# Strassen's scheme for the merge gates of a decoder layer, with the gates kept in DRAM and the up projections turned round

## The chip, the core and the metric

The kernel runs on one core of a Trainium2 chip. The core has a matrix engine (TensorE; PE in the profile, PEld its weight loads), a vector engine (VectorE, DVE), a scalar engine (ScalarE, ACT), a general one (GpSimd, POOL) and a queue engine (SyncE, SP) that here only starts transfers; POOL starts some as well. Each runs its own instructions in the order in which the program issues them; they meet at semaphores. On-chip memory has 128 partitions. Matmul results arrive in eight banks of 128 x 512 float32 values, which the kernel names in four kinds of two: g, s, t, o. The metric is the device time of one execution, in microseconds (us).

## The reference

512 tokens, 2048 channels, one layer. What matters here:

```python
h = rms_norm(x, norm_g[l])
proj = h @ w_in[l]
q, kv, g_logits, z_a, uv, z_b, merge_logits = jnp.split(proj, SPLIT_IDX, axis=-1)
...
o_a = nsa_attention(q, ...) * jax.nn.silu(z_a)                       # 1024 wide
o_b = spatial_gating(uv, ...) * jax.nn.silu(z_b)                     # 1024 wide
g_a, g_b = jnp.split(jax.nn.sigmoid(merge_logits), 2, axis=-1)       # 2048 wide each
merged = g_a * (o_a @ w_up_a[l]) + g_b * (o_b @ w_up_b[l])
x = x + merged @ w_out[l]
x = x + jax.nn.sigmoid(x @ w_ple_gate[l]) * (p[l] @ w_ple[l])
return rms_norm(x, final_g)
```

`merge_logits` is the product of h (512 x 2048) with the last 4096 columns of `w_in`: the largest product of the layer.

## The kernel before

Every projection is a `Job`, and one generator, `gemm` (L170), issues the matmuls of all jobs in the order in which `add_job` listed them. `fill(n)` lets it go n yields further, `finish(name)` until a job is done. Float32 is kept by a split: each operand is a high part (rounded to the matmul's type) and a low part (the rest), and each product is three matmuls: high x high, high x low, low x high. Weights come by SP's queue in 512 KB loads into a ring of three (`raw`, L137); ScalarE casts the high part (`high`, L98, from L150), VectorE subtracts for the low part (`low`, L104, from L162), in pieces ("subs") of 128 x 512. `split_to` does this two subs ahead of the matmuls (`state["ahead"]`), the cast one more. The buffers of high parts are four, of low parts three.

A job of kind "T" has 128 columns of weights as the stationary operand and all 512 tokens moving: its result has channels on partitions. A sub holds four blocks of 128 rows (`per_sub`), so 4 x 3 = 12 matmuls. A job of kind "N" has 128 tokens stationary and 512 columns of weights moving: tokens on partitions, a sub is one block of rows, four token tiles, again 12 matmuls.

Two lists carry other work. What stands in `deferred` is issued at the next `flush()`. What stands in `background` is taken off one or two entries (`state["pops"]`) at each sub, after the split of the sub two ahead and before the matmuls of the present one.

The stages in order: PLE products and norms; keys, values and compression; attention, with q and za jobs woven in; then vn (L410), u (L412) and zb (L414) for the gated MLP; then for each of 16 blocks of 128 channels the gates `ma`, `mb` (2048 deep) and the up projections `ua`, `ub` (1024 deep) (L457 to L461); `wo`; `pg`. o_a is split into `oa_h`, `oa_l` after the attention (background, L967), o_b into `ob_h`, `ob_l` by `evac_zb` (L399). The gate's sigmoid is taken as tanh, with the factor 0.5 applied later: `evac_gate` (L426) puts tanh into `sig` tiles, `evac_up` (L447) forms (tanh + 1) x product on VectorE and adds the two branches on POOL into `m32` (channels on partitions), and `merged_split` (L438) splits that into `act_h`, `act_l`, which until then held h. `x2` is the same memory as `m32`, reloaded from x.

In the u stage the work is ordered by hand: the layer norm's pieces (`aggregate` and eight `affine`, L1009) go through `background`, one per sub, until the list is empty (L1025); then after each u job the four spatial-gating matmuls (L1034), the add on VectorE (L1037) and the multiplication on POOL (L1039), with `fill(3)` in between.

Of the kernel before, what the change touches and what calls it, by code (L numbers as in the profile page):

```python
# [20 lines left out]
P = 128  # L21
# [15 lines left out]
class Job:  # L37
# [5 lines left out]

    def __init__(self, name, kind, w, c0, cols, kt, act, evac, banks=None, tail=0):
        self.name, self.kind, self.w, self.c0, self.cols, self.kt = name, kind, w, c0, cols, kt
        self.act, self.evac, self.banks, self.tail = act, evac, banks, tail
        self.per_sub = max(1, 512 // cols)
        self.per_load = 2 * self.per_sub


@with_exitstack
def kernel(ctx: ExitStack, tc: tile.TileContext, x, p, norm_g, w_in,
# [67 lines left out]

    def add_job(job):
        first = 0
        while first < job.kt:
            n = min(job.per_load, job.kt - first)
            loads.append((job, first, n))
            for k in range(first, first + n, job.per_sub):
                subs.append((job, k, min(job.per_sub, first + n - k), len(loads) - 1))
            first += n
        jobs.append(job)

    raw, parts = {}, {}
    state = {"loads": 0, "high": 0, "low": 0, "ahead": 0, "more": 1, "pops": 2}

    def load_to(i):
        while state["loads"] <= min(i, len(loads) - 1):
            job, k0, n = loads[state["loads"]]
            t = stream.tile([P, n, job.cols], F32, tag="raw", name="raw")  # L137
            nc.sync.dma_start(t, job.w[k0 * P:(k0 + n) * P, job.c0:job.c0 + job.cols]
                              .rearrange("(k p) c -> p k c", p=P))
            raw[state["loads"]] = (t, k0)  # L140
            state["loads"] += 1

    def split_to(i, more=1):
        while state["high"] <= min(i + more, len(subs) - 1):
            job, k, n, li = subs[state["high"]]
            t, k0 = raw[li]
            if k >= job.kt - job.tail:
# [3 lines left out]
            src = t[:, k - k0:k - k0 + n]  # L151
            high(hi, src)
            parts[state["high"]] = [hi, None, src]
            state["high"] += 1
        while state["low"] <= min(i, len(subs) - 1):
            job, k, n, li = subs[state["low"]]
            pt = parts[state["low"]]
            if k >= job.kt - job.tail:
# [5 lines left out]
            li = subs[state["low"] - 1][3]  # L164
            if state["low"] == len(subs) or subs[state["low"]][3] != li:
                load_to(li + 3)
# [3 lines left out]
    def gemm():  # L170
        si = 0
        for job in jobs:
            if job.kind == "T":
# [162 lines left out]
    spill = dram.tile([S, D], F32, name="spill")  # L336

# [61 lines left out]
    def evac_zb(ft):  # L399
        def f(ps):  # L400
# [5 lines left out]
            split(ob_h[:, ft], ob_l[:, ft], t, 0.5)  # L406
# [9 lines left out]
    oa = {}  # L416

    def oa_act(k):
        return oa["h"][:, k], oa["l"][:, k]

    def ob_act(k):
        return ob_h[:, k], ob_l[:, k]

    merge_tiles = {}

    def evac_gate(f, n):  # L426
# [9 lines left out]
    split_done = set()  # L436

    def merged_split(f):  # L438
        def e():
            split(act_h[:, f], act_l[:, f], merge_tiles["m"][:, f], 0.5)  # L440
            split_done.add(f)
            if len(split_done) == KT:
                for tt in range(TT):
                    nc.gpsimd.dma_start(x2[:, tt], x[tt * P:tt * P + P])
        return e

    def evac_up(f, n):  # L447
        def e(ps):
            t = merge_tiles[n]
            nc.vector.scalar_tensor_tensor(out=t, in0=t, scalar=1.0, in1=ps, op0=ALU.add, op1=ALU.mult)  # L450
            if n == 1:
# [656 lines left out]
```

## Time and profile before

| | |
|---|---|
| median of 3 runs | 1649.08 us (1649.03 to 1649.33) |
| the profiled execution, in all | 1649.7 us |
| its span, first to last instruction | 1648.0 us |
| granted TensorE clock, mean over the span | 0.998 |
| bytes moved | 168.02 MB, 102 GB/s on average |
| u jobs begin / zb jobs begin | 579.0 / 673.2 us |
| gates and up projections begin / wo begins | 760.4 / 1282.4 us |

The span is shorter than an execution by what lies around the first and the last instruction. A line of a group gives its source line, engine, operation, output and inputs, shapes and count, then busy time and the mean of one, then the engine's idle time ahead of it and what ended most of that. Matmuls overlap, so the duration of one is not its cost: cost is a stretch of the span divided by the matmuls in it.

### The profile page before, as it was taken

The numbers are of one execution on the slowest core, as the hardware profiler recorded it, in microseconds if no ns is written. First come the engines' busy times: TensorE is split into PE (matmuls) and PEld (weight loads), VectorE is DVE, ScalarE is ACT, GpSimd is POOL, SyncE is SP. The second block draws the span as 40 slices with busy tenths as digits, with TensorE's granted clock in tenths as the row PEclk, the third lists the DMA queues.
The fourth block names the chain that finished last, engine by engine and source line by source line (L and its number), as shares of the span: only waits on it lengthen the run. The fifth ranks groups of instructions, "written<-read, shape, count | busy, mean of one in ns | idle before, by whom it ended". The sixth has DMA issues, their size and how long they took to land.

```text
span 1648.0 us, 20570 instructions
## 1 busy us (share of the span) xinstructions
PE 1634.8 (99%) x7821; PEld 1368.2 (83%) x7821; DVE 748.7 (45%) x1500; ACT 616.5 (37%) x1241; POOL 114.6 (7%) x145
## 2 busy tenths in 40 slices
PE   9999999999999999999999999999999999999997
PEld 8889988888888888888888888888888888888886
DVE  6544378988873363343322222223223433333335
ACT  6433356666653232233222222222223322223335
POOL 1200000110120001000000000000000000000001
PEclk9999999999999999999999999999999999999999
DMA  8422421122124333343333333333333533363333
GB/s 318 128 80 72 118 64 47 44 52 52 41 63 145 99 90 90 90 102 94 98 102 90 103 92 101 97 95 102 90 102 91 203 90 93 100 217 95 98 102 128
DMA packets 217202, 168.02 MB, mean 102 GB/s; under 512 B 4992, under 2 KB 190992, under 8 KB 215568
## 3 DMA queue, kind: packets, MB, share of 16 engines
q1 hardware_dynamic: 213488, 151.57, 32.9%
q0 software_dynamic: 3472, 14.79, 2.4%
q8 instruction: 61, 1.00, 0.3%
q10 hardware_dynamic: 144, 0.36, 0.1%
q14 instruction: 37, 0.30, 0.1%
HBM read 158.31 MB, written 8.39 MB: 101 GB/s over the span
## 4 chain that ended last, share of the span: by engine, by line
PE 96%; DVE 2%; ACT 1%; issue 0%; POOL 0%; DVEq 0%; POOLq 0%; ACTq 0%
PE ps_wo L202 4%; PE ps_ma L192 4%; PE ps_mb L192 4%; PE ps_mb L191 4%; PE ps_ma L191 4%; PE ps_mb L190 4%; PE ps_ma L190 4%; PE ps_wo L203 4%; PE ps_wo L204 4%; PE ps_pg L204 3%; PE ps_pg L202 3%; PE ps_pg L203 3%; PE ps_za L190 2%; PE ps_za L192 2%; PE ps_t L815 2%; PE ps_za L191 2%
## 5 line engine op out<-in xcount | busy, mean ns | idle before, releaser
L104 DVE TENSOR_TENSOR lo<-raw,hi 128x512 fp32r<-128x512 f32 (+1 forms) x536 | 366.9, 688 | 651.9 <-PE ps_mb L192 127.4
L98 ACT CAST hi<-raw 128x512 fp32r<-128x512 f32 (+1 forms) x536 | 328.2, 615 | 732.4 <-PE ps_wo L204 105.9
L202 PE MATMUL ps_wo<-hi,act_h 128*128 128x512 f32 x256 | 100.2, 392 | 0.1
L204 PE MATMUL ps_wo<-hi,act_l 128*128 128x512 f32 x256 | 99.6, 389 | 0.0
L203 PE MATMUL ps_wo<-lo,act_h 128*128 128x512 f32 x256 | 99.6, 389 | 0.0
L190 PE MATMUL ps_ma<-act_h,hi 128*128 128x512 f32 x256 | 99.6, 389 | 0.0
L191 PE MATMUL ps_ma<-act_l,hi 128*128 128x512 f32 x256 | 99.6, 389 | 0.0
L192 PE MATMUL ps_ma<-act_h,lo 128*128 128x512 f32 x256 | 99.6, 389 | 0.0
L190 PE MATMUL ps_mb<-act_h,hi 128*128 128x512 f32 x256 | 99.6, 389 | 0.0
L191 PE MATMUL ps_mb<-act_l,hi 128*128 128x512 f32 x256 | 99.6, 389 | 0.0
L192 PE MATMUL ps_mb<-act_h,lo 128*128 128x512 f32 x256 | 99.6, 389 | 0.0
L98 ACT CAST pth<-ps_t 128x512 fp32r<-128x512 f32 (+1 forms) x88 | 47.9, 544 | 65.7 <-PE ps_t L815 65.4
L776 ACT ACTIVATE prob<-prob,st 128x512 f32<-128x512 f32 (+3 forms) x128 | 70.7, 555 | 4.0 <-DVE st L767 3.8
L452 POOL TENSOR_TENSOR m<-sig,sig 128x512 f32<-128x512 f32 x16 | 27.0, 1686 | 582.3 <-DVE sig L450 464.2
L104 DVE TENSOR_TENSOR ptl<-ps_t,pth 128x512 fp32r<-128x512 f32 (+1 forms) x88 | 56.3, 639 | 21.1 <-ACT pth L98 20.2
L767 DVE CUSTOM_DVE_ANT_0 prob<-ps_s,b 128x512 f32<-128x512 f32 (+3 forms) x128 | 56.3, 486 | 10.1 <-PE ps_s L764 9.9
L202 PEld LDWEIGHTS ps_wo<-hi,act_h 128*128 128x128 f32 x256 | 48.1, 188 | 10.3 <-DVE sig L450 0.5
L191 PEld LDWEIGHTS ps_ma<-act_l,hi 128*128 128x128 f32 x256 | 48.0, 188 | 10.0
L191 PEld LDWEIGHTS ps_mb<-act_l,hi 128*128 128x128 f32 x256 | 48.0, 188 | 10.0
L204 PEld LDWEIGHTS ps_wo<-hi,act_l 128*128 128x128 f32 x256 | 48.0, 188 | 10.0
L190 PEld LDWEIGHTS ps_ma<-act_h,hi 128*128 128x128 f32 x256 | 48.0, 188 | 10.0
L190 PEld LDWEIGHTS ps_mb<-act_h,hi 128*128 128x128 f32 x256 | 48.0, 188 | 10.0
(311 smaller groups left out, 3684.6 us busy)
## 6 DMA issues: line engine op xcount, KB each, us to landing
raw<-in_w_in_dram SPq DMA_DIRECT2D x164, 512.0 KB, 3.7
raw<-in_w_out_dram SPq DMA_DIRECT2D x32, 512.0 KB, 3.6
raw<-in_w_ple_gate_dram SPq DMA_DIRECT2D x32, 512.0 KB, 3.6
raw<-in_w_up_a_dram SPq DMA_DIRECT2D x16, 512.0 KB, 3.8
raw<-in_w_up_b_dram SPq DMA_DIRECT2D x16, 512.0 KB, 3.7
xt<-in_x_dram SPq DMA_DIRECT2D x4, 1024.0 KB, 9.5
spill<-ple POOLq DMA_DIRECT2D x4, 1024.0 KB, 8.2
m<-in_x_dram POOLq DMA_DIRECT2D x4, 1024.0 KB, 7.8
```

The lines of the kernel that those rows point to most:

```text
L98: nc.scalar.copy(hi, src)
L104: nc.vector.tensor_tensor(out=lo, in0=src, in1=hi.bitcast(F32), op=ALU.subtract)
L190: nc.tensor.matmul(ps, hi[:, j], ah, start=st, stop=False)
L191: nc.tensor.matmul(ps, hi[:, j], al, start=False, stop=False)
L192: nc.tensor.matmul(ps, lo[:, j], ah, start=False, stop=sp)
L202: nc.tensor.matmul(o, ah[:, sl], hi[:, j], start=st, stop=False)
L203: nc.tensor.matmul(o, ah[:, sl], lo[:, j], start=False, stop=False)
L204: nc.tensor.matmul(o, al[:, sl], hi[:, j], start=False, stop=sp)
L452: nc.gpsimd.tensor_tensor(out=merge_tiles["m"][:, f], in0=merge_tiles[0], in1=t, op=ALU.add)
L767: nc.vector.tensor_tensor_reduce(out=pt[:, j * n:j * n + n], in0=o[:, j], in1=b0[:, 512 - n:], scale=-SLOPE[h], scalar=3.0e38, op0=ALU.add ...
L776: nc.scalar.activation(sl, sl, AF.Exp, bias=st[:, 0, j, hh:hh + 1], scale=-1.0, accum_out=st[:, 1, j, hh:hh + 1])
L815: nc.tensor.transpose(b[:, (2 * e + hh) * P:(2 * e + hh + 1) * P], pts[hh][:, c:c + P], ident)
```

## The change

The gates become four jobs of a new kind "S", each 1024 columns of `w_in` for all 512 tokens. With h cut into four quarters (tokens 0 to 255 and 256 to 511, rows 0 to 1023 and 1024 to 2047) and the weights likewise, the job forms seven products of quarters in place of eight (Strassen's scheme in Winograd's form). Each product has four subs of two row blocks (`PRODUCTS`), each 2 x 2 x 3 = 12 matmuls with 512 moving columns, and a sub's weights are 128 x 2 x 512.

- Weight sums: VectorE forms the differences in place (`sum_to`), one sub ahead of the split. Loads go into rings b11 and b12 (four each) and `raw`; they start no sooner than the new pool `quad` is open, which is after the u stage.
- Activation sums: `sum_chunk`, four chunks of nine pieces, is put in `background` after the layer norm's pieces. S1 and S2 go to `ob_h`, `ob_l`; S3 and S4 are staged and written to DRAM by POOL's queue, and read back after zb7, S3 into the quarter of `act_h`, `act_l` that is no longer needed. What is left in the list after the last u job is issued at once.
- Results: `evac_gates` copies products 1, 5 and 6 with ScalarE, adds with VectorE, takes tanh two flushes later and writes the gates to DRAM by POOL's queue.
- o_a and o_b are written to DRAM when they are formed and read back for the up projections (o_a into `ob_h`, `ob_l` during the last gate job, o_b into new tiles).
- Up projections: eight "N" jobs of 512 columns in the order a0 a1 b0 b1 a2 a3 b2 b3. `evac_up` takes the gates from tiles loaded with `load_gate`; POOL adds. `turn_merged` transposes a column group on TensorE (16 transposes) and splits it into `act_h`, `act_l`, ten yields of the following job after `ub` has ended.
- x is loaded into `x2` after the last of these; the banks of wo and pg change places.

```diff
...
+PRODUCTS = [(p, j) for pair in ("15", "63", "7", "24") for j in range(4) for p in pair]
+BANK_OF = {"1": 0, "6": 0, "7": 0, "4": 0, "5": 1, "3": 1, "2": 2}
...
+            for p, j in PRODUCTS:
+                last = {"7": ("b11",), "4": ("b12", "b21"), "3": ("b22",)}.get(p, ())
+                for tag in last:
+                    last_sub[ld[tag, j]] = len(subs)
+                subs.append((job, p, j, ld))
...
+    def load_next():
+        while state["loads"] < len(loads):
+            b = before[state["loads"]]
+            if b is not None and last_sub[b] >= state["low"]:
+                return
+            if loads[state["loads"]][0] != "raw" and "pool" not in quad:
+                return
+            load_to(state["loads"])
...
+    def sum_to(i):
+        while state["sum"] <= min(i, len(subs) - 1):
+            job, p, j, ld = subs[state["sum"]]
+            state["sum"] += 1
+            if job.kind != "S" or p not in "5674":
+                continue
+            b = {tag: raw[ld[tag, j]] for tag in ("b11", "b12") + {"6": ("b22",), "4": ("b21",)}.get(p, ())}
+            o, x, y = {"5": ("b12", "b12", "b11"), "6": ("b12", "b22", "b12"),
+                       "7": ("b11", "b12", "b11"), "4": ("b12", "b21", "b12")}[p]
+            nc.vector.tensor_tensor(out=b[o], in0=b[x], in1=b[y], op=ALU.subtract)
...
+        sum_to(i + 1)
...
+            if job.kind == "S":
+                sets = {}
+                for p, j in PRODUCTS:
+                    flush()
+                    split_to(si + state["ahead"])
+                    for _ in range(state["pops"]):
+                        if background:
+                            background.popleft()()
+                    hi, lo, _ = parts.pop(si)
+                    si += 1
+                    b = BANK_OF[p]
+                    if b not in sets:
+                        sets[b] = [bank(job.banks[b], f"ps_{job.name}{b}{t}") for t in range(2)]
+                    for i in range(2):
+                        k = 2 * j + i
+                        st, sp = k == 0 and p in "152", k == 7
+                        for t in range(2):
+                            o = sets[b][t]
+                            ah, al = job.act(p, k, t)
+                            go = p not in "152"
+                            nc.tensor.matmul(o, ah, hi[:, i], start=st, stop=False, skip_group_check=go)
+                            nc.tensor.matmul(o, ah, lo[:, i], start=False, stop=False, skip_group_check=go)
+                            nc.tensor.matmul(o, al, hi[:, i], start=False, stop=sp, skip_group_check=go)
+                            if not (i and t):
+                                yield
+                    if j == 3:
+                        job.evac(p, sets[b])
+                    if (p, j) == ("4", 3):
+                        done.add(job.name)
+                    yield
+                continue
...
-            split(ob_h[:, ft], ob_l[:, ft], t, 0.5)
+            o = quad["pool"].tile([P, 2, 512], F32R, tag="ls", name="ob", bufs=3)
+            split(o[:, 0], o[:, 1], t, 0.5)
+            nc.gpsimd.dma_start(ob_dram[:, :, ft], o)
...
+    gate_dram = [dram.tile([S, D], F32, name=f"gate{n}") for n in range(2)]
+    def gate_act(p, k, t):
+        sl = slice(t * P, t * P + P)
+        if p in "124":
+            k, sl = k + 8 * (p != "1"), slice(t * P + 256 * (p == "4"), t * P + 256 * (p == "4") + P)
+            return act_h[:, k, sl], act_l[:, k, sl]
+        if p == "7":
+            sl = slice(t * P + 256, t * P + 256 + P)
+            return act_h[:, k, sl], act_l[:, k, sl]
+        o = {"5": ob_h, "6": ob_l}[p] if p in "56" else quad["s4"]
+        return o[:, k, sl], o[:, k, t * P + 256:t * P + 256 + P]
+    def evac_gates(n, c0):
+        keep = {}
+        def put(t, c, tile, src):
+            nc.scalar.activation(tile, src, AF.Tanh, scale=0.5)
+            nc.gpsimd.dma_start(gate_dram[n][t * P:t * P + P, c0 + c:c0 + c + 512], tile)
+        def later(f):
+            deferred.append(lambda: deferred.append(f))
+        def e(p, ps):
+            if p in "156":
+                tag, pool, bufs = {"1": ("s1", quad["pool"], 2), "5": ("hi", stream, 4), "6": ("lo", stream, 3)}[p]
+                keep[p] = [pool.tile([P, 512], F32, tag=tag, name="keep" + p, bufs=bufs) for _ in range(2)]
+                for t in range(2):
+                    nc.scalar.copy(keep[p][t], ps[t])
+            elif p in "372":
+                other, row, c = {"3": ("6", 0, 512), "7": ("5", 2, 512), "2": ("1", 0, 0)}[p]
+                for t in range(2):
+                    o = keep[other][t]
+                    nc.vector.tensor_tensor(out=o, in0=ps[t], in1=o, op=ALU.add)
+                    later(lambda o=o, t=t: put(row + t, c, o, o))
+            else:
+                for t in range(2):
+                    put(2 + t, 0, quad["pool"].tile([P, 512], F32, tag="c21", name="c21", bufs=2), ps[t])
+        return e
+    for q, (c, n) in enumerate(((0, 0), (0, 1), (1024, 0), (1024, 1))):
+        add_job(Job(f"m{q}", "S", w_in, C_M + D * n + c, 512, KT, gate_act, evac_gates(n, c),
+                    (("o", "t", "s"), ("g", "t", "s"))[q % 2]))
+    up_tiles = {}
+    def load_gate(n, cg):
+        t = up_tiles[n, cg] = up_tiles["pool"].tile([P, TT, 512], F32, tag="gate", name="gate", bufs=4)
+        nc.gpsimd.dma_start(t, gate_dram[n][:, 512 * cg:512 * cg + 512].rearrange("(t p) c -> p t c", p=P))
+    def evac_up(n, cg):
         def e(ps):
-            t = tmp_pool["p"].tile([P, S], F32, tag=f"sig{n}", name=f"sig{n}")
-            nc.scalar.activation(t, ps, AF.Tanh, scale=0.5)
-            merge_tiles[n] = t
-            if f == KT - 1 and n == 1:
-                for i in range(KT - 1):
-                    background.append(merged_split(i))
+            g = up_tiles[n, cg]
+            for t in range(TT):
+                nc.vector.scalar_tensor_tensor(out=g[:, t], in0=g[:, t], scalar=1.0, in1=ps[t],
+                                               op0=ALU.add, op1=ALU.mult)
+                if n == 1:
+                    m = up_tiles[0, cg]
+                    nc.gpsimd.tensor_tensor(out=m[:, t], in0=m[:, t], in1=g[:, t], op=ALU.add)
         return e
...
-    for f in range(KT):
-        add_job(Job(f"ma{f}", "T", w_in, C_M + 128 * f, 128, KT, h_act, evac_gate(f, 0)))
...
+    for i, s in enumerate("a0 a1 b0 b1 a2 a3 b2 b3".split()):
+        n, cg = "ab".index(s[0]), int(s[1])
+        add_job(Job("u" + s, "N", (w_up_a, w_up_b)[n], 512 * cg, 512, 8, (oa_act, ob_act)[n], evac_up(n, cg),
+                    (ys, xs)[i % 2]))
...
+    def store_oa(ft):
+        o = sums.tile([P, 2, S], F32R, tag="stage", name="oa", bufs=6)
+        split(o[:, 0], o[:, 1], o32[:, ft], 0.5)
+        nc.gpsimd.dma_start(oa_dram[:, :, ft], o)
+    def sum_chunk(c):
+        lo_t, hi_t = slice(0, 256), slice(256, 512)
+        k1, k2 = slice(2 * c, 2 * c + 2), slice(2 * c + 8, 2 * c + 10)
+        h11, l11, h21, l21 = (a[:, k1, t] for t in (lo_t, hi_t) for a in (act_h, act_l))
+        h12, l12, h22, l22 = (a[:, k2, t] for t in (lo_t, hi_t) for a in (act_h, act_l))
+        w = {}
+        def op(a, b, f):
+            nc.vector.tensor_tensor(out=w["t"], in0=a.bitcast(F32) if a is not None else w["t"],
+                                    in1=b.bitcast(F32) if b is not None else w["t"], op=f)
+        def first():
+            w["t"] = sums.tile([P, 2, 256], F32, tag="sum", name="sum", bufs=2)
+            op(h21, h22, ALU.add)
+            op(None, l21, ALU.add)
+        def s1():
+            op(None, l22, ALU.add)
+            split(ob_h[:, k1, lo_t], ob_h[:, k1, hi_t], w["t"])
+        def s2():
+            op(None, h11, ALU.subtract)
+            op(None, l11, ALU.subtract)
+            high(ob_l[:, k1, lo_t], w["t"])
+        def s2_low():
+            low(ob_l[:, k1, lo_t], ob_l[:, k1, hi_t], w["t"])
+        def staged():
+            w["o"] = sums.tile([P, 2, S], F32R, tag="stage", name="stage", bufs=6)
+            high(w["o"][:, :, lo_t], w["t"])
+        def s4():
+            op(h12, None, ALU.subtract)
+            op(None, l12, ALU.add)
+            staged()
+        def s4_low():
+            low(w["o"][:, :, lo_t], w["o"][:, :, hi_t], w["t"])
+            nc.gpsimd.dma_start(s4_dram[:, k1], w["o"])
+        def s3():
+            w["t"] = sums.tile([P, 2, 256], F32, tag="sum", name="sum", bufs=2)
+            op(h11, h21, ALU.subtract)
+            op(None, l11, ALU.add)
+        def s3_high():
+            op(None, l21, ALU.subtract)
+            staged()
+        def s3_low():
+            low(w["o"][:, :, lo_t], w["o"][:, :, hi_t], w["t"])
+            for i, t in enumerate((lo_t, hi_t)):
+                nc.gpsimd.dma_start(s3_dram[:, i, k1], w["o"][:, :, t])
+        return [first, s1, s2, s2_low, s4, s4_low, s3, s3_high, s3_low]
...
+        for ft in range(8):
+            background.append(lambda ft=ft: store_oa(ft))
...
+                fill(1)
+        for c in range(4):
+            background.extend(sum_chunk(c))
+        for g in range(8):
+            finish(f"u{g}")
...
+        while background:
+            background.popleft()()
+    quad["pool"] = ph_q.enter_context(tc.tile_pool(name="quad", bufs=1))
...
+    state["pops"] = 2
+    ph_uz.close()
+    ph_s4 = ExitStack()
+    quad["s4"] = ph_s4.enter_context(tc.tile_pool(name="s4p", bufs=1, side="right")).tile([P, 8, S], F32R, name="s4")
+    nc.gpsimd.dma_start(quad["s4"], s4_dram)
+    for i, a in enumerate((act_h, act_l)):
+        nc.gpsimd.dma_start(a[:, 0:8, 256:512], s3_dram[:, i])
+    for q in range(3):
+        finish(f"m{q}")
+    fill(4 * 8)
+    nc.gpsimd.dma_start(ob_h, oa_dram[:, 0])
+    fill(4 * 8)
+    nc.gpsimd.dma_start(ob_l, oa_dram[:, 1])
+    finish("m3")
+    ph_q.close()
+    ph_s4.close()
+    obp = ctx.enter_context(tc.tile_pool(name="obp", bufs=1))
     fp = ctx.enter_context(tc.tile_pool(name="fp", bufs=1))
     f_tiles["ss"] = fp.tile([P, TT, 4], F32, name="ss")
-    with tc.tile_pool(name="sigp", bufs=2) as sigp:
-        tmp_pool["p"] = sigp
-        finish(f"ub{KT - 1}")
-    free_banks = {0: "gs", 1: "to", 2: "gs", 3: "to"}
+    for n, i in enumerate("hl"):
+        ob2[i] = obp.tile([P, 8, S], F32R, name="ob2" + i)
+    ph_up = ExitStack()
+    up_tiles["pool"] = ph_up.enter_context(tc.tile_pool(name="gatep", bufs=1))
+    load_gate(0, 0)
+    load_gate(0, 1)
+    for n, i in enumerate("hl"):
+        nc.gpsimd.dma_start(ob2[i], ob_dram[:, n])
+    load_gate(1, 0)
+    load_gate(1, 1)
...
+    def turn_merged(cg, banks, n):
+        for j in (0, 2):
+            pair = [bank(banks[i], "ps_m") for i in range(2)]
+            for i, b in enumerate(pair):
+                for t in range(TT):
+                    c = (j + i) * P
+                    nc.tensor.transpose(b[:, t * P:t * P + P], up_tiles[0, cg][:, t, c:c + P], ident)
+            for i, b in enumerate(pair):
+                k = 4 * cg + j + i
+                split(act_h[:, k], act_l[:, k], b, 0.5)
+            fill(n)
+    for a in (0, 2):
+        finish(f"ub{a}")
+        fill(10)
+        turn_merged(a, "to", 6)
+        if a == 0:
+            load_gate(0, 2)
+            load_gate(1, 2)
+        finish(f"ub{a + 1}")
+        fill(10)
+        turn_merged(a + 1, "gs", 6)
+        if a == 0:
+            load_gate(0, 3)
+            load_gate(1, 3)
+    ph_up.close()
+    mp = ctx.enter_context(tc.tile_pool(name="mp", bufs=1))
+    x2 = mp.tile([P, TT, D], F32, name="x2")
+    for t in range(TT):
+        nc.gpsimd.dma_start(x2[:, t], x[t * P:t * P + P])
...
```

More of the change, by code (lines that the diff above doesn't have):

```diff
@@ L457 @@
[L457 to L466 removed]
+        return ob2["h"][:, k], ob2["l"][:, k]
@@ L968 @@
+    ph_uz = ExitStack()
+    ph_q = ExitStack()
     with tc.tile_pool(name="mlp", bufs=1) as mlp:
```

229 lines of the change are left out of this document (113 added, 116 removed).

## The prediction

> **What bounds the kernel now.** First the page: busy time by engine and the chain that ended last; then the list of what PE waited for.
>
> ```profile
> span 1648.0 us, 20570 instructions
> PE 1634.8 (99%) x7821; PEld 1368.2 (83%) x7821; DVE 748.7 (45%) x1500; ACT 616.5 (37%) x1241; POOL 114.6 (7%) x145
> PE 96%; DVE 2%; ACT 1%; issue 0%; POOL 0%; DVEq 0%; POOLq 0%; ACTq 0%
> PE ps_spin L576 <- POOL eps_t L74: 1.4, 1, 1.4
> PE ps_t L815 <- DVE ptl L104: 1.2, 1, 1.2
> ```
>
> TensorE is the bound from end to end: in the whole span the two longest waits of PE are 1.4 and 1.2 us. A matmul taken away is time gained, unless a wait appears. So the question is how many matmuls go, and which new wait reaches PE. A busy PE does not tell what a matmul costs, so next come the stretch of gates and up projections, the output projection after it, and one group of matmuls (columns of the windows: length, then busy time and count of PE, PEld, DVE, ACT, POOL, then clock, DMA share, GB/s).
>
> ```profile
> 760.40:1282.40 522.00, 522.00 (x2305) 432.23 (x2304) 158.43 (x234) 140.34 (x234) 25.28 (x15) 1.00 0.36 97
> 1282.40:1462.20 179.80, 179.70 (x817) 149.02 (x816) 67.62 (x100) 50.60 (x84) 3.82 (x5) 1.00 0.37 118
> L190 PE MATMUL ps_ma<-act_h,hi 128*128 128x512 f32 x256 | 99.6, 389 | 0.0
> 25.76 0.87 PE ps_x L591 x8
> L1077 PE MATMUL ps_x<-ident,m 128*128 128x128 f32 x64 | 8.3, 272 | 0.0
> ```
>
> The mean of 389 ns is a latency; matmuls overlap. By the code the first stretch holds 16 x (48+48+24+24) = 2304 matmuls, so one costs 522.0 / 2304 = 0.2266 us. A transpose costs 0.87 / 8 = 0.109 us in a run of eight. The second stretch checks both: 768 matmuls and 48 transposes make 174.0 + 5.2 = 179.2 of 179.8 us. The unit of all that follows is a "step": 12 matmuls on one piece of weights, 12 x 0.2266 = 2.72 us.
>
> **Removed and added on PE.** The gates were 32 jobs of 16 x 3 = 1536 matmuls. Each of the four new jobs runs 28 steps of 12, 336 matmuls, 1344 in all: 192 fewer, 192 x 0.2266 = **-43.5 us**. The up projections keep their 768 with the operands' roles exchanged, and the second stretch prices that form alike. With tokens on partitions the merged rows must be turned: 64 transposes at 0.109 = **+7.0 us** (at 8.3 / 64 = 0.130, the mean that the lines give, 8.3).
>
> **VectorE and ScalarE in the new gate stage.** A step's weights are now 1024 elements wide per partition, not 512, and 16 of a job's 28 steps have a weight difference on VectorE before the split.
>
> ```profile
> L104 DVE TENSOR_TENSOR lo<-raw,hi 128x512 fp32r<-128x512 f32 x520 | 359.3, 695 | 632.9 <-PE ps_mb L192 127.4 <-PE ps_ma L192 95.3 <-issue 93.1
> L104 DVE TENSOR_TENSOR lo<-raw,hi 128x304 fp32r<-128x304 f32 x16 | 7.6, 475 | 19.1 <-PE ps_vw L203 14.1 <-PE ps_vs L203 4.6 <-issue 0.4
> L98 ACT CAST hi<-raw 128x512 fp32r<-128x512 f32 x520 | 321.1, 621 | 711.1 <-PE ps_wo L204 105.9 <-PE ps_ma L191 97.9 <-PE ps_pg L204 91.5
> L98 ACT CAST hi<-raw 128x304 fp32r<-128x304 f32 x16 | 7.2, 447 | 21.3 <-PE ps_vw L204 14.2 <-PE ps_vs L204 7.1
> ```
>
> From 304 to 512 elements a VectorE subtraction grows by 0.220 us, so 1024 take about 0.695 + 512/208 x 0.220 = 1.24 us; a ScalarE cast 0.621 + 0.43 = 1.05. Per job VectorE has 28 lows, 16 differences and six adds of 0.69: 44 x 1.24 + 4.1 = 58.7 us against 28 x 2.72 = 76.2 on PE, or 77%. The tightest place is product 7 (a difference and a low in each step, 2.48 of 2.72) with two result adds in front, which wait for PE and hold the lows behind them: adds 1.4, difference 1.24, low 1.24 end 3.9 us into a step whose low is wanted 5.4 us in. The steps run two ahead, so I charge **0**. At the first job's third step the low stands behind the last zb evacuation (three VectorE operations around two ScalarE ones, about 3.4 us) and a difference: 3.4 + 2.5 = 5.9 against 5.4, **+0.4**.
>
> **The sums of the activations.** These are 36 small pieces of background work, put in the list when the layer norm's own are through; each step of the u jobs takes one off, and after the last u job the rest is emitted at once.
>
> ```profile
> L190 PE MATMUL ps_u<-act_h,hi x128: 389/389/476, 579.0 to 671.8; 128*128 128x512 f32 x128
> L1012 DVE SCALAR_TENSOR_TENSOR vn<-vn,mv,lg x8: 745/746/748, 588.0 to 607.1; 128x512 f32<-128x512 f32 x8
> ...
> 673.24 0.48 PE L190 MATMUL ps_zb<-act_h,hi 128*128 128x512 f32 x1
> 673.52 0.69 DVE L1037 TENSOR_TENSOR vn<-ps_sv,bs 128x512 f32<-128x512 f32 x1 [2.86 <-PE ps_sv L1034]
> 674.13 0.68 DVE L104 TENSOR_TENSOR lo<-raw,hi 128x512 fp32r<-128x512 f32 x1
> 676.31 0.69 DVE L104 TENSOR_TENSOR lo<-raw,hi 128x512 fp32r<-128x512 f32 x1 [1.50 <-issue]
> ```
>
> The eight affines (L1012) come 2.73 us apart: one piece per step. The last is at 607.1, (607.1 - 579.0) / 2.72 = 10 steps after u0 began. From step 11 to the end of u7 (step 31) that leaves 21 pieces, and one goes with zb0's first step. **Fourteen of 36 remain**, and are issued in a row ahead of the low of zb0's fourth step. In them are 21 VectorE operations of 512 elements and 6 casts on ScalarE, each cast with its low right behind it. What these cost in a row, from dependent operations and a wait for ScalarE elsewhere:
>
> ```profile
> 292.27 0.69 DVE L886 TENSOR_TENSOR cs<-cs,c 128x512 f32<-128x512 f32 x1
> 292.99 0.69 DVE L887 TENSOR_REDUCE cst<-cs 128x16 f32<-128x512 f32 x1
> 293.71 0.69 DVE L888 TENSOR_TENSOR cs<-cs,cst 128x512 f32<-128x512 f32 x1
> ...
> 500.68 1.30 DVE L106 SCALAR_TENSOR_TENSOR oa_l<-o,oa_h 128x512 fp32r<-128x512 f32 x2 [0.77 <-ACT oa_h L100]
> ```
>
> Dependent ones follow at 0.72 us, independent ones at about 0.61 (two in 1.30), and one that waits for a cast of its input about 0.77 after the operation before it ended, 1.46 from start to start. So 9 x 0.72 + 6 x 0.61 + 6 x 1.46 = 18.9 us. In the rows above VectorE starts the low of zb0's third step at 674.13, one more piece to 675.35, then the burst to 694.25, then the low that PE wants, to 694.9. PE has three steps in hand from 673.24 and needs that low two matmuls into the fourth, at 681.85: **+13.1 us**. Bounds: 17.3 us for the burst (all at 0.61) gives 11.5; with VectorE also blocked by POOL seven times (its multiply and six stores; 1.1 us each, the longest L106, 1.804 against 0.686) 20.8. I stay with 13.1, the nearest rows. The 22 pieces taken singly are about 1.9 us in a 2.72 us step beside one low of 0.69: hidden, with two steps of cover.
>
> ```profile
> L106 DVE SCALAR_TENSOR_TENSOR act_l<-m,act_h x16: 678/686/1804, 1273.6 to 1293.2; 128x512 fp32r<-128x512 f32 x16
> 1.43 3.78 PE ps_spin L576 x16
> 1642.00:1643.00 1.00, 0.00 (x0) 0.00 (x0) 0.89 (x4) 0.54 (x1) 0.00 (x0) 0.76 0.01 0
> 1643.00:1644.00 1.00, 0.00 (x0) 0.00 (x0) 0.53 (x2) 0.35 (x1) 0.00 (x0) 0.50 0.08 32
> ```
>
> An idle PE loses its clock: after the last matmul near 1638.7 the granted clock falls to a half within 1642 to 1643, about 3.8 us on, so a wait of 13 us would end at half clock. The way back shows at the start: 16 spins take 3.78 us, 0.236 each against 0.109, and full pace is there before 10 us. 3.8 to 7 us at half pace lose 1.9 to 3.5; I take **+2.0**. The Trainium skill, "TensorE: Matmul & The Clock Gate", section on the HAM clock gate, says the clock returns after about 3.4 us of sustained work; by it an estimate of 1.7 us, and the sum would be 0.3 us lower. The fall agrees with its idle window of 3.4 us.
>
> **Merge and the way through DRAM.** POOL's four adds per column group follow the evacuation, and the code gives them 10 x 3 matmuls, 6.8 us, before the transposes.
>
> ```profile
> L450 DVE SCALAR_TENSOR_TENSOR sig<-sig,ps_ub 128x512 f32<-128x512 f32 x16 | 11.0, 688 | 30.0 <-PE ps_ub L192 30.0
> L452 POOL TENSOR_TENSOR m<-sig,sig x16: 1552/1696/1697, 794.1 to 1283.6; 128x512 f32<-128x512 f32 x16
> L505 POOL TENSOR_TENSOR m<-m,fg x12: 1287/1288/1727, 1512.0 to 1619.1; 128x512 f32<-128x512 f32 x12
> raw<-in_w_in_dram SPq DMA_DIRECT2D x164, 512.0 KB, 3.7
> m<-in_x_dram POOLq DMA_DIRECT2D x4, 1024.0 KB, 7.8
> ple<-spill POOLq DMA_DIRECT2D x4, 1024.0 KB, 13.3
> 1290.00:1295.00 5.00, 5.00 (x23) 4.14 (x23) 3.81 (x6) 2.69 (x5) 0.53 (x1) 1.00 1.01 395
> 1295.00:1300.00 5.00, 5.00 (x23) 4.14 (x23) 1.31 (x2) 1.03 (x2) 0.00 (x0) 1.00 1.02 399
> ```
>
> The chain is 0.9 + 4 adds of 1.29 to 1.70 = 6.1 to 7.7 us: 0 to 0.9 us per group, four groups, I take **+1.5** (0 to 4). The transfers: 20 MB go out to DRAM and back on POOL's queue. The first four loads after the gates (two gate tiles, both halves of o_b, 6 MB) must land before ub0, 16 steps or 43.5 us after ua0 begins. The four loads of x (m) ran at 395 to 399 GB/s with the weights among them, and PE was busy throughout. 6 MB over the 300 GB/s left by the weights is 20 us: **0**. s4 (2 MB, some 5 us after zb7) is wanted 9 steps, 24 us, into the first gate job: 2 x 7.8 + 5 = 21, hidden but close. Weight bytes are the same; a weight piece takes 3.7 us and is ordered about 10 us ahead: 0.
>
> **Sum.** 1648.0 - 43.5 + 7.0 + 0.4 + 13.1 + 2.0 + 1.5 = 1628.5 span. The profiled execution took 1649.7 in all, the median of the runs shown is 1649.08, 1.1 above the span: **1629.6 us**, own range 1626 to 1643 from the bounds above.
>
> **Rivals.** (a) The burst does not reach PE, because the pieces run out earlier or VectorE's lead is longer: 13.1 + 2.0 drop out, 1614.5. For it: VectorE is busy 45%. Against: the counted steps. (b) The DRAM way replaces the wait: if POOL's loads run one behind another at 13.3 us per MB, as ple is listed, 6 MB take 80 us, ub0 waits 36, and the time is about 1666. It turns slower from 63 us (10.5 per MB) on. Against: the 395 GB/s. (c) VectorE sets the pace of the gate stage: if the difference, cast and low of a step run as one chain (1.24 + 1.05 + 1.24 + handoffs = 3.7 us), 64 steps lose 1.0 each, 1694. It turns slower above 0.3 us per step. Against: the next step's difference is issued before this step's low, and three buffers each.
>
> **How the numbers follow.** Forecast 0.70, (a) 0.11, (b) 0.07, (c) 0.07, the rest 0.05 near no change. 0.2% is 3.3 us: faster 0.81, same 0.05, slower 0.14. The range 1612 to 1645 holds (a) and the forecast's own, and leaves out the slow rivals.
>
> **What would show it.** 1344 gate matmuls at 0.2266; one PE wait of 11 to 16 us early in zb, released by a VectorE low, with half clock behind it; waits of under 1 us in front of the new transposes, released by POOL; none at ub0 or inside the gate stage. No such wait in zb, or several us lost per gate job, would make it wrong.

## The result, and the profile after

| | before | after |
|---|---|---|
| median | 1649.2 us (4 runs, 1649.03 to 1649.63) | 1630.04 us (4 runs, 1629.33 to 1630.70) |
| ratio after / before | | 0.9883, 95% interval 0.9866 to 0.9900 |
| span of the profiled execution | 1648.0 us | 1629.0 us |
| bytes moved | 168.02 MB | 209.97 MB |

The kernel is 1.2% faster. The forecast was 1629.6. The profile of the changed kernel, its page first (span, busy time by engine, chain that ended last):

```profile
span 1629.0 us, 20503 instructions
PE 1601.3 (98%) x7693; PEld 1340.1 (82%) x7693; DVE 929.1 (57%) x1628; ACT 677.3 (42%) x1265; POOL 157.6 (10%) x219
PE 95%; DVE 3%; ACT 1%; issue 0%; DMA 0%; DVEq 0%; ACTq 0%
```

TensorE is still the bound: 128 instructions fewer (192 matmuls gone, 64 transposes more). But VectorE's share of the chain has gone from 2% to 3%. The list of what PE waited for says where (engine, what it worked on, releaser; total, times, longest):

```profile
PE ps_zb L298 <- DVE lo L111: 13.8, 1, 13.8
PE ps_spin L709 <- POOL eps_t L81: 1.4, 1, 1.4
PE ps_t L948 <- DVE ptl L111: 1.2, 1, 1.2
...
PE ps_m L269 <- DVE ls L111: 0.2, 1, 0.2
```

One wait is new, in zb, and it is ten times the next. The wait of the gate stage (ps_m) is 0.2 us. Transposes and `ub0` do not appear. The stages as windows (columns as in the prediction) are zb, the gates, and the up projections with their transposes:

```profile
673.40:777.30 103.90, 90.07 (x387) 73.98 (x386) 53.77 (x77) 30.53 (x51) 10.25 (x14) 0.92 0.59 174
777.30:1082.50 305.20, 305.01 (x1346) 252.23 (x1345) 223.59 (x203) 146.38 (x168) 19.18 (x34) 1.00 0.46 150
1082.50:1262.00 179.50, 179.50 (x818) 149.13 (x817) 73.28 (x106) 47.66 (x80) 28.12 (x27) 1.00 0.51 171
```

Gates and up projections together took 522.0 us and now take 305.2 + 179.5 = 484.7: 37.3 us gained. The forecast's terms for the 192 matmuls and the 48 transposes that lie in these windows make 43.5 - 5.2 = 38.3. zb took 760.4 - 673.2 = 87.2 and now takes 103.9: 16.7 us given back, against 13.1 + 2.0 = 15.1. At the wait itself PE's timeline (start, duration, instruction, idle before it and its releaser) and VectorE's read:

```profile
681.87 0.39 PE L297 MATMUL ps_zb<-act_l,hi 128*128 128x512 f32 x1
696.09 0.80 PE L298 MATMUL ps_zb<-act_h,lo 128*128 128x512 f32 x1 [13.83 <-DVE lo L111]
```

```profile
674.27 0.68 DVE L111 TENSOR_TENSOR lo<-raw,hi 128x512 fp32r<-128x512 f32 x1
674.87 1.78 DVE L111 TENSOR_TENSOR ob_l<-sum,ob_l 128x512 fp32r<-128x512 f32 x1
676.69 0.69 DVE L1110 TENSOR_TENSOR sum<-act_h,sum 128x512 f32<-128x512 f32 x1
...
694.74 0.69 DVE L111 TENSOR_TENSOR stage<-sum,stage 128x512 fp32r<-128x512 f32 x1 [0.68 <-ACT stage L105]
695.35 1.89 DVE L111 TENSOR_TENSOR lo<-raw,hi 128x512 fp32r<-128x512 f32 x3
```

Between the low at 674.27 and the lows at 695.35 VectorE does nothing but sums of activations (`ob_l`, `sum`, `stage`). PE's next matmul was due 0.227 us after 681.87, at 682.10, and came at 696.09: 14.0 us late (the list counts 13.8, from the end of the matmul before).

### The profile page after: what moved, and what is told of

The parts are those of the page before. It is cut to its first block, busy times and chain, and to the rows that moved or that the text cites. A ratio compares the mean times of both kernels' runs of the same rounds, so it can differ in the third digit from the quotient of the medians.

```text
span 1629.0 us, 20503 instructions
## 1 busy us (share of the span) xinstructions
PE 1601.3 (98%) x7693; PEld 1340.1 (82%) x7693; DVE 929.1 (57%) x1628; ACT 677.3 (42%) x1265; POOL 157.6 (10%) x219
## 2 busy tenths in 40 slices
DMA packets 158115, 209.97 MB, mean 129 GB/s; under 512 B 6192, under 2 KB 97984, under 8 KB 155840
## 4 chain that ended last, share of the span: by engine, by line
PE 95%; DVE 3%; ACT 1%; issue 0%; DMA 0%; DVEq 0%; ACTq 0%
PE ps_m L269 6%; PE ps_m L268 6%; PE ps_m L270 6%; PE ps_wo L309 4%; PE ps_wo L310 4%; PE ps_wo L308 4%; PE ps_pg L308 3%; PE ps_pg L309 3%; PE ps_pg L310 3%; PE ps_t L948 2%; PE ps_za L296 2%; PE ps_za L298 2%; PE ps_za L297 2%; PE ps_ub L310 2%; PE ps_ua L310 2%; PE ps_u L296 2%
## 5 line engine op out<-in xcount | busy, mean ns | idle before, releaser
L111 DVE TENSOR_TENSOR lo<-raw,hi 128x512 fp32r<-128x512 f32 (+1 forms) x408 | 280.5, 694 | 412.1 <-PE ps_pg L309 84.0
L105 ACT CAST hi<-raw 128x512 fp32r<-128x512 f32 (+1 forms) x408 | 248.3, 614 | 514.3 <-PE ps_wo L310 109.8
L111 DVE TENSOR_TENSOR ls<-b,hs 128x1024 fp32r<-128x1024 f32 x80 | 98.0, 1225 | 66.9 <-ACT hs L105 66.7
L105 ACT CAST hs<-b 128x1024 fp32r<-128x1024 f32 x80 | 84.1, 1052 | 94.8 <-PE ps_m L270 91.5
L269 PE MATMUL ps_m<-ls,act_h 128*128 128x512 f32 x256 | 99.7, 390 | 0.2 <-DVE ls L111 0.2
L268 PE MATMUL ps_m<-hs,act_h 128*128 128x512 f32 x256 | 99.6, 389 | 0.0
L270 PE MATMUL ps_m<-hs,act_l 128*128 128x512 f32 x256 | 99.6, 389 | 0.0
L298 PE MATMUL ps_zb<-act_h,lo 128*128 128x512 f32 x128 | 51.2, 400 | 13.8 <-DVE lo L111 13.8
L269 PEld LDWEIGHTS ps_m<-ls,act_h 128*128 128x128 f32 x256 | 48.1, 188 | 10.5 <-DVE ls L111 0.6
L296 PE MATMUL ps_za<-act_h,hi 128*128 128x512 f32 x128 | 55.8, 436 | 0.0
```

The costliest lines, as they stand in the source:

```text
L105: nc.scalar.copy(hi, src)
L111: nc.vector.tensor_tensor(out=lo, in0=src, in1=hi.bitcast(F32), op=ALU.subtract)
L268: nc.tensor.matmul(o, ah, hi[:, i], start=st, stop=False, skip_group_check=go)
L269: nc.tensor.matmul(o, ah, lo[:, i], start=False, stop=False, skip_group_check=go)
L270: nc.tensor.matmul(o, al, hi[:, i], start=False, stop=sp, skip_group_check=go)
L296: nc.tensor.matmul(ps, hi[:, j], ah, start=st, stop=False)
```

## The experiments

Each is the changed kernel with one edit. "+" and "-" times are against its 1630.04 us. A time with a range beside it is the median of four executions, one without is of a single execution.

### The wait in zb: is it the row of leftover pieces?

**Half of the sums earlier.** Two of the four chunks go into the list behind `ph_o.close()`, ahead of the layer norm's pieces, and only two after them, so that none is left over:

```diff
+        for c in range(2):
+            background.extend(sum_chunk(c))
...
-        for c in range(4):
+        for c in range(2, 4):
             background.extend(sum_chunk(c))
```

> Two of the four chunks of activation sums go into the background list before the vn jobs, the other two stay; nothing is left to be issued at once after the last u job. Theory (the row of pieces on VectorE makes PE wait in zb, and the half clock follows from that wait): the 14.0 us wait and some 2.7 us at half pace go, 1630.0 - 16.7 = 1613.3 us, and zb0 to zb7 take 87.2 us again as before the change. Rival (VectorE has too little room in the vn and u stages, so that the same work makes PE wait there instead): no nearer than 1625 us, with PE waits released by VectorE before 673 us. Rival (the wait in zb is from the weights or from DRAM traffic): unchanged, 1630 us.

Measured: 1614.32 us (1613.92 to 1614.61), ratio to the kernel before 0.9784 (0.9770 to 0.9799). The windows of u, zb and the gates, then the new row of its list of waits:

```profile
579.00:674.20 95.20, 95.20 (x454) 79.95 (x453) 65.39 (x92) 32.66 (x55) 15.21 (x13) 1.00 0.43 115
674.20:761.10 86.90, 86.90 (x386) 71.96 (x386) 38.08 (x55) 27.11 (x45) 6.38 (x8) 1.00 0.61 183
761.10:1066.30 305.20, 305.01 (x1346) 252.21 (x1345) 223.55 (x203) 146.34 (x168) 19.21 (x34) 1.00 0.44 150
```

```profile
PE ps_vn L308 <- ACT vn L493: 0.4, 1, 0.4
```

The wait is gone, zb is 86.9 us long at full clock, 17.0 less, and the gate stage is the same to 0.1 us. A little is given back ahead of it: zb begins 0.8 us later (674.2 against 673.4), with a new wait of 0.4 us in vn. By the medians the net gain is 15.7 us, and this version beats both kernels. That one sum is formed beside other work and the same sum in a row stops PE is the difference.

**All 36 pieces in a row** (none taken off in the u stage):

```diff
             background.extend(sum_chunk(c))
+        state["pops"] = 0
```

> No piece is taken off during the u jobs; all 36 are issued in a row after the last u job. Theory (the wait is the length of the row on VectorE less PE's lead): a chunk in a row is 5 x 0.72 + 3 x 0.61 + 5... by the rule of the prediction about 12.6 us, four make 50.4 us in place of 18.9 and one piece of 0.6, so the wait grows by 30.9 us: 1661 us, wait about 45 us. Rival (the wait is one fixed stall at the change of stage, from memory that is freed late): the same 14 us, 1630 us.

Measured: 1661.54 us, +31.5, and in its list of waits:

```profile
PE ps_zb L298 <- DVE lo L111: 44.6, 1, 44.6
```

The wait follows the number of pieces: 14 give 13.8 us and 36 give 44.6, (44.6 - 13.8) / 22 = 1.4 us for each further piece. The 22 pieces taken singly in the u stage cost nothing there; moved into the row they cost 30.8 us.

### The half clock behind the wait

**PE kept busy in its wait.** Matmuls on the identity, whose result nobody reads, are issued right behind the row of pieces, which on PE is behind zb's first nine matmuls; 124 in one kernel and 60 in the other:

```diff
+        spin2 = bank("o", "ps_spin2")
+        for _ in range(124):
+            nc.tensor.matmul(spin2[:, :P], ident, ident, start=True, stop=True)
```

> The pieces stay in a row, but 124 matmuls of 128 columns without use (0.109 us each, 13.5 us) are issued on PE just behind the row of pieces, so that PE works while VectorE does the pieces. Theory (half pace in zb follows from PE's idle time): PE still gets its low at about 696 us, but at full clock: 1630.0 - 2.7 = 1627.3 us, no clock below 1.0 in zb. Rival (the slow matmuls after the wait come from the weight traffic that piled up, not from idleness): the same half pace, 1630 us. Rival (the low comes sooner than thought): the matmuls without use add time, above 1633 us.

Measured with 124: 1641.48 us (1640.92 to 1642.19), a miss of 14 us. PE's timeline shows why:

```profile
676.27 27.86 PE L1241 MATMUL ps_spin<-ident 128*128 128x128 f32 x248
```

One such matmul in full precision is two instructions, 0.225 us instead of the 0.109 that I had taken from a transpose of the same width. The spins outlast the wait by 27.9 - 14.0 = 13.9 us. With no wait and no half clock the sum is +27.9 - 14.0 - 2.7 = +11.2, and +11.4 was measured; but the run does not isolate the clock. So with 60, 13.5 us:

> As the run with matmuls without use, but 60 of them: each turned out to be two instructions of 0.112 us, so 60 make 13.5 us, just less than the wait. Theory (half pace in zb follows from PE's idle time): the low still comes at about 696 us, PE is never idle for more than 1 us and keeps its clock: 1630.0 - 2.7 = 1627.3 us, zb 101.2 us long and not 103.9. Rival (half pace comes from the weights that piled up): 1630 us and the same half pace.

Measured: 1627.56 us (1627.16 to 1627.68), -2.5. Its zb stage, useless matmuls included:

```profile
672.70:774.00 101.30, 100.90 (x507) 85.50 (x506) 53.78 (x77) 30.56 (x51) 10.26 (x14) 1.00 0.60 179
```

The stage is 101.3 us long where it was 103.9. The clock stays at 1.00, and that alone is worth 2.5 us: a kernel that does useless work is faster than the one that waits. The half pace comes from the idleness, not from VectorE's or the transfers' load, which are the same (53.78 us against 53.77, DMA share 0.60 against 0.59).

### Is a matmul taken away worth its 0.2266 us?

**An eighth product.** The third product's matmuls are issued twice, so the quarter that it goes into holds it twice; loads, splits and evacuations stay at seven.

```diff
-                    for i in range(2):
+                    for i in (0, 1, 0, 1) if p == "3" else (0, 1):
```

> The matmuls of product 3 are issued twice (one result quarter is then wrong by that product): 192 more matmuls in the four gate jobs, as many as eight products would have, with the same loads, splits, sums and results. Theory (PE sets the pace of the gate stage, so the saving is the matmuls alone): 192 x 0.2266 = 43.5 us more, 1673.5 us, the gate stage 305.2 + 43.5 = 348.7 us. Rival (part of the gate stage is paced by VectorE or the loads, so that saved matmuls are worth less): less than 35 us more.

Measured: 1676.60 us, +46.6, 3.1 more than expected, with a wait that the changed kernel does not have:

```profile
PE ps_m L268 <- DMA ob_l<-oa_d: 2.7, 1, 2.7
```

The edit adds yields. `fill(4 * 8)` counts yields, so the reload of `ob_l` with o_a moved forward, ahead of the last step of product 6 in the last gate job, which then waits for it (and reads o_a in place of its sum). Without that wait it is 46.6 - 2.7 = 43.9. The same again with the yields of the doubled half left out:

```diff
+                    for r, i in enumerate((0, 1, 0, 1) if p == "3" else (0, 1)):
...
-                            if not (i and t):
+                            if r < 2 and not (i and t):
```

> An eighth product in each gate job, without the extra places for other work that the first kernel with one had: the third product's matmuls are issued twice (one quarter of each result is then wrong), and nothing else is moved. Theory: 192 matmuls of 0.2266 us come back, 43.5 us, and no wait of TensorE on a transfer: gate stage 348.7 us instead of 305.2, time about 1673.5 us. Rival: the eighth product is partly hidden in idle time of TensorE that the trace does not show, time under 1668 us. Rival: the 2.7 us wait for the reload of the other activation's two halves is there again, time about 1676 us, and then it does not come from the places.

Measured: 1673.89 us, +43.9, without the wait; the gate stage is

```profile
777.30:1126.00 348.70, 348.51 (x1538) 288.26 (x1537) 224.24 (x203) 146.62 (x168) 19.18 (x34) 1.00 0.39 132
```

348.7 - 305.2 = 43.5 us, to the tenth the price of 192 matmuls. TensorE is the only bound of this stage, and the second run shows that the excess of the first came from where the work was placed.

### How near is VectorE to the pace of the gate stage?

**Low parts made twice**, in every gate sub, and in those of products 1, 2 and 3 alone, which need no difference of weights:

```diff
             low(*pt)
+            if job.kind == "S":
+                low(*pt)
```

(`if job.kind == "S" and k in "123"` in the second.)

> Every low of the gate jobs is computed twice (same values): 28 more VectorE operations of 1.24 us per job. Theory (VectorE is hidden in the gate stage up to PE's 76.2 us per job, now 58.7): 58.7 + 34.7 = 93.4 us per job, so VectorE becomes the bound and the stage grows by 4 x 17.2 = 69 us: 1699 us. Rival (each step's chain of difference, cast and low sets the pace, with little room left already): the whole 34.7 per job would show, +139 us, 1769 us. Rival (VectorE has far more room than reckoned): below 1660 us.

> Only the lows of products 1, 2 and 3 are computed twice (12 of 28 steps, those without a difference): 58.7 + 14.9 = 73.6 us of VectorE per job against 76.2 of PE. Theory (room of 17 us per job behind PE): within 5 us of 1630 us. Rival (little room): 4 x 14.9 = 60 us more, 1690 us.

Measured: 1680.13 us (+50.1) and 1631.26 us (+1.2). The first's gate stage, its group of lows, and PE's waits for them, a fence for each view:

```profile
777.20:1132.10 354.90, 326.17 (x1346) 246.84 (x1346) 349.44 (x313) 148.51 (x168) 19.36 (x34) 1.00 0.40 129
```

```profile
L111 DVE TENSOR_TENSOR ls<-b,hs 128x1024 fp32r<-128x1024 f32 x160 | 194.1, 1222 | 2.7
```

```profile
PE ps_m L271 <- DVE ls L111: 26.8, 61, 1.7
```

VectorE is now busy 349.4 of 354.9 us (98%) and sets the pace. The stage is 49.7 us longer; 68.5 was my count of VectorE's work (58.7 + 28 x 1.24 = 93.4 us per job, four jobs, against 305.2). Two terms of that count are too high. The work of a job before the edit is 223.59 / 4 = 55.9 us, not 58.7. And the 110 further lows in this window (313 - 203; two of the 112 lie before it) added 349.44 - 223.59 = 125.9 us, 1.14 each, less than the 1.222 that one lasts, so they overlap. So the miss is in my count; that the wall exists, and that the stage reaches it only with over a third more VectorE work (305.2 / 223.6 = 1.36), stands. The second run adds 48 of the 112 and loses nothing in that stage but two waits of 1.9 us in all.

### The merge: does POOL's chain lie beside the matmuls?

**The transposes 8 x 3 matmuls sooner:**

```diff
-        fill(10)
+        fill(2)
```

(in front of both calls of `turn_merged`)

> The transposes of a merged group come 2 yields (6 matmuls) behind the end of ub, not 10. The trace of the changed kernel shows the evacuation starting 2.0 us before the job's last matmul (token tile 0 is complete first), and the last add on POOL ending 6.7 us after that start. Theory: PE waits 6.7 + 0.1 - 2.0 - 1.4 = 3.4 us less the first transposes' 0.3, four times: 12 to 14 us more, 1642 to 1644 us. Rival (the reading of the prediction, evacuation after the job's end): 6.1 to 7.7 less 1.4, four times, and half clock after waits that long: 1650 us or more.

Measured: 1646.05 us, +16.0, over the 12 to 14 expected. The window of the up projections up to the start of `wo`, the row of waits, PE's timeline in the first group and the second, and windows of 2 us, three in the first and one in the second:

```profile
1082.00:1273.10 191.10, 184.40 (x817) 151.62 (x816) 72.81 (x106) 47.63 (x80) 26.69 (x27) 0.98 0.47 160
```

```profile
PE ps_m L1282 <- POOL gate L596: 8.9, 8, 1.3
```

```profile
1150.51 0.33 PE L1282 MATMUL ps_m<-ident,gate 128*128 128x128 f32 x1 [1.34 <-POOL gate L596]
1151.73 1.33 PE L1282 MATMUL ps_m<-ident,gate 128*128 128x128 f32 x5 [0.89 <-POOL gate L596]
...
1158.05 1.04 PE L1282 MATMUL ps_m<-ident,gate 128*128 128x128 f32 x8
1158.84 0.48 PE L308 MATMUL ps_ub<-hi,ob2h 128*128 128x512 f32 x1
...
1176.64 0.49 PE L1282 MATMUL ps_m<-ident,gate 128*128 128x128 f32 x2
1178.47 0.33 PE L1282 MATMUL ps_m<-ident,gate 128*128 128x128 f32 x1 [1.34 <-POOL gate L596]
1179.69 0.77 PE L1282 MATMUL ps_m<-ident,gate 128*128 128x128 f32 x5 [0.89 <-POOL gate L596]
1180.21 0.48 PE L308 MATMUL ps_ua<-hi,ob_h 128*128 128x512 f32 x1
```

```profile
1150.00:1152.00 2.00, 0.60 (x3) 0.41 (x4) 0.00 (x0) 0.00 (x0) 1.70 (x3) 0.93 0.00 0
1152.00:1154.00 2.00, 2.00 (x8) 1.81 (x8) 0.97 (x2) 1.19 (x2) 0.74 (x1) 0.50 0.33 37
1154.00:1156.00 2.00, 2.00 (x8) 1.54 (x8) 1.11 (x2) 0.51 (x1) 0.00 (x0) 0.72 0.86 334
...
1178.00:1180.00 2.00, 0.64 (x4) 0.45 (x5) 0.00 (x0) 0.00 (x0) 1.70 (x3) 1.00 0.00 0
```

This stretch, with three of the four groups, is 191.1 - 179.5 = 11.6 us longer; the fourth group lies at the start of `wo`. Two waits in each group, of 1.34 and 0.89 us, make 8.9 in all. They hold PE for longer than they last: from the first transpose of the second group to the next matmul of the job it is 1180.21 - 1176.64 = 3.57 us, and 1158.84 - 1158.05 = 0.79 for eight transposes without a wait. That is 2.78 us for each group, 8.3 for the three. The other 3.3 are half clock (the clock is the last but two of the columns), some 1.7 us in the first group and in the third; in the second the same two waits left the clock at 1.00. The fourth has the waits and the half clock once more. So the chain on POOL is hidden by the `fill(10)`, and that cover is worth some 16 us.

**The transposes twice:**

```diff
-                for t in range(TT):
+                for t in (0, 1, 2, 3, 0, 1, 2, 3):
```

> Each of the 64 transposes of the merged gates is issued twice into the same place (same result). Theory: each costs TensorE 0.109 us and nothing else, since its input is complete 2.1 us before and the splits after it lie beside the up projections' matmuls: 64 x 0.109 = 7.0 us, time about 1637 us. Rival: transposes of full-precision data cost what the 128-column full-precision matmuls of the second experiment cost, 0.225 us, or the splits then come late: 14 us or more, time 1644 us or above. Rival: part of them lies in idle time, under 1634 us.

Measured: 1637.26 us, +7.2, with no new wait; the up projections, with 48 of the 64 in them:

```profile
1082.50:1267.30 184.80, 184.80 (x866) 154.44 (x865) 74.24 (x107) 48.15 (x80) 28.55 (x28) 1.00 0.49 167
```

184.8 - 179.5 = 5.3 us for 48 more, 0.110 each. The transposes are on PE's path at the price forecast.

## Why the prediction was right

**Matmuls, -43.5.** Right: 43.5 in the stage of the run that puts them back.

**Transposes, +7.0.** Right: 5.3 for 48, which makes 7.1 for 64.

**The row of 14 pieces, +13.1.** Right in mechanism and place (PE stops at zb0's fourth step, released by a low of VectorE), 0.9 short: 14.0. The row ended 1.1 us later than counted (the next low at 695.35 against 694.25), and the single piece ahead of it shows why: its last operation, at 674.87, took 1.78 us instead of 0.69, while POOL multiplied.

```profile
674.52 1.58 POOL L1234 TENSOR_TENSOR uz<-uz,vn 128x512 f32<-128x512 f32 x1 [8.63 <-DVE vn L1232]
```

The prediction had blocking by POOL in its upper bound and not in its value. (That POOL is the cause is read from the overlap in time; no run took its multiplication away.) The row's own operations were costed rightly, from dependent and independent ones elsewhere. That the wait can be blamed on VectorE's 57% is excluded: the first experiment has the same operations on an equally busy engine and no wait.

**Half clock, +2.0.** Right in mechanism, 2.7 in this execution by the stage's length (16.7 - 14.0), 3.0 by the 6.1 us that PE ran at half pace. The term is not a constant; see the last section.

**POOL's adds before the transposes, +1.5.** This value was wrong, its lower bound right: 0. I counted the chain from the end of the `ub` job. A token tile has its own bank, and the first bank is complete nine matmuls earlier. VectorE, then POOL and PE:

```profile
1146.06 2.73 DVE L592 SCALAR_TENSOR_TENSOR gate<-gate,ps_ub 128x512 f32<-128x512 f32 x4 [0.16 <-PE ps_ub L310]
```

```profile
1146.84 5.95 POOL L596 TENSOR_TENSOR gate<-gate 128x512 f32<-128x512 f32 x4 [51.61 <-DVE gate L592]
1154.70 1.03 PE L1282 MATMUL ps_m<-ident,gate 128*128 128x128 f32 x8
```

The adds end at 1146.84 + 5.95 = 1152.8, and PE's transposes begin at 1154.7: 1.9 us in hand, where 0 to 0.9 us of lateness were charged. The price of the missing cover was underrated as well: the run with `fill(2)` lost more to the clock than I expected.

**VectorE and ScalarE in the gate stage, 0, and +0.4 at the first job.** Right: 0.2 us of wait. The durations at 1024 elements were extrapolated as 1.24 and 1.05:

```profile
L111 DVE TENSOR_TENSOR ls<-b,hs 128x1024 fp32r<-128x1024 f32 x80 | 98.0, 1225 | 66.9 <-ACT hs L105 66.7
L105 ACT CAST hs<-b 128x1024 fp32r<-128x1024 f32 x80 | 84.1, 1052 | 94.8 <-PE ps_m L270 91.5 <-DVE b L204 2.7 <-ACT hs L105 0.6
```

They measure 1.225 and 1.052, and VectorE is busy 223.6 of 305.2 us, 73% where 77% was reckoned. Rival (c), a chain of difference, cast and low that paces the stage, falls: the steps overlap, and VectorE decides only with over a third more work.

**The way through DRAM, 0.** Right. Rival (b) had POOL's loads one behind another at 13.3 us per MB. The transfers (KB each, us from issue to landing), then the timeline of POOL and PE:

```profile
ob2h<-ob_d POOLq DMA_DIRECT2D x1, 2048.0 KB, 14.1
ob2l<-ob_d POOLq DMA_DIRECT2D x1, 2048.0 KB, 19.3
```

```profile
1093.12 0.58 POOL L1272 DMA_DIRECT2D ob2l<-ob_d  x1
...
1126.14 0.39 PE L308 MATMUL ps_ub<-hi,ob2h 128*128 128x512 f32 x1
```

Both 2 MB tiles are on their way together: the second was ordered at 1093.1 and had landed 19.3 us later, at 1112.4, and `ub0` begins at 1126.1. That is 13.7 us in hand; this cover was not taken away in any run, so what it is worth was not measured.

**The sum.** -43.5 + 7.0 + 14.0 + 2.7 + 0.2 = -19.6 from 1648.0 makes 1628.4 for a span of 1629.0; 0.6 us are not assigned. The forecast's terms were off by +0.9, +0.7, -1.5 and -0.2, which nearly cancel: that 0.4 us remain in the end is luck, since the terms were known less well than that.

## What to carry to other kernels

Here TensorE was busy 98%, and the matmuls taken from it paid in full. The question was which queue of another engine now held something that it needs: a list of small pieces that was harmless one per step became a stop, as long as the row less TensorE's lead, when the remainder was issued at once in front of a needed operation. Count the pieces against the steps that are there to take them, and start the list early enough (here 15.7 us for an edit of three lines). In an experiment that adds instructions, look for what else is placed by counting them, and price them from a row of the very same operation and type.

## What the runs showed of the hardware that was not expected

**Half clock lasts a whole number of 3.41 us.** Windows around the fall and the return of the granted clock, in the changed kernel:

```profile
684.00:686.00 2.00, 0.00 (x0) 0.00 (x0) 1.28 (x3) 0.62 (x1) 0.00 (x0) 0.77 0.92 225
...
702.00:704.00 2.00, 2.00 (x10) 1.64 (x9) 1.07 (x3) 0.97 (x2) 0.00 (x0) 0.96 0.03 8
```

and in the kernel with the lows of products 1, 2 and 3 made twice, whose zb stage is the same program:

```profile
684.00:686.00 2.00, 0.00 (x0) 0.00 (x0) 1.28 (x3) 0.62 (x1) 0.00 (x0) 0.86 0.93 229
...
698.00:700.00 2.00, 2.00 (x8) 1.64 (x7) 0.00 (x0) 0.00 (x0) 0.00 (x0) 0.73 1.04 270
```

A mean of 0.77 over 2 us means full clock for (0.77 - 0.5) / 0.5 x 2 = 1.08 us, so the fall is at 685.08; the return, likewise, at 702.16. That is 17.08 us, five times 3.416. The second kernel falls at 685.44 and returns at 699.08: 13.64, four times 3.41. Worked out alike, the row of all 36 pieces gives 47.76 (14 times 3.411), and the first group of the kernel with early transposes 3.40 (once). PE resumed at 696.1 in the first two: after that it ran 6.1 us at half clock in one execution and 3.0 in the other. The Trainium skill, "TensorE: Matmul & The Clock Gate", section "What's actually happening", says that activity is judged in windows of 3413 ns that run freely, without regard to the kernel; the four intervals agree. In the same section the Trainium skill gives about 3.4 us of sustained work for the return, which lies between the 3.0 and the 6.1 us measured here. A term for half clock behind a wait is therefore a range, here 1.5 to 3 us, and no edit is to be judged by a difference of that size from a single execution, such as the +1.2 us above.

**Two short waits can halve the clock, or leave it.** With early transposes the same pair of waits, 1.34 and 0.89 us with three transposes between, came four times. The clock fell in the first, third and fourth group, at 1151.72, 1250.72 and 1278.0, and stayed at 1.00 in the second. The falls lie 99.0 and 27.3 us apart, 29 and 8 times 3.41. In the 3.41 us that ended in a fall PE had waited 2.2, 1.9 and 2.2 us. In the second group, where windows counted on from the first fall end at 1179.03 inside the second wait, the most is 1.34 + 0.23 = 1.6. That fits windows that run freely, but no run here moved the waits alone. In the run with all lows twice, waits of up to 1.7 us left the clock at 1.00 throughout the gate stage.
